# Expert weights of a mixture-of-experts stage: half of the raw pieces read into activation tiles, a strips read and a count sum moved to later places

## The chip, the cores and the metric

The kernel runs on one core of a Trainium2 chip. The metric is device time in microseconds for one launch, the median of several runs. The profile is of one execution on the same kind of chip; all positions in it are microseconds from the start of its span.

## The reference

Two transformer blocks run one after the other on 512 tokens of width 1024 (attention, recurrences and MLPs in the first; a delta-net layer and a sparse-attention layer in the second). Each of the two layers of the second block ends in a mixture of experts. This is the part that matters here:

```python
def hier_moe(x, w_grp, b_grp, w_rt, b_rt, w_gate, w_up, w_down):
    ...
    grp_prob, grp_idx = lax.top_k(grp_p, 1)
    ...
    top_p, top_i = lax.top_k(jax.nn.softmax(e_logits, axis=-1), MOE_TOP_K)
    ...
    def step(acc, e_in):
        wg, wu, wd, ge = e_in
        hdn = jax.nn.silu(xt @ wg) * (xt @ wu)
        return acc + ge[:, None] * (hdn @ wd).astype(jnp.float32), None

    y, _ = lax.scan(step, jnp.zeros((b * t, d), jnp.float32), (w_gate, w_up, w_down, gate.T))
```

There are 16 experts in 4 groups; each token goes to two experts of one group. The hidden width of an expert is 256.

## The kernel before, in words

**Numbers as pairs.** Matrix products are made from split numbers. `piece` (line 123) reads a raw piece of weights, 128 x 1024 f32 or 0.5 MB, into a raw tile (`ws`), ScalarE copies it to the rounded half `wh` (line 130), VectorE subtracts to get the rest `wl` (line 131), and `mm3` (line 148) makes three matmuls (lines 151 to 153) for each 128 x 128 block. A raw tile is free again when the subtraction is done. `wap` (line 135) yields the blocks of all pieces of a weight matrix in order.

**Tiles.** Tiles are taken by tag, each tag with a number of buffers (`BUFS`, line 17):

```python
BUFS = {"t": 6, "x": 16, "h": 4, "y": 10, "P": 3, "PT": 3, "bc": 2, "ws": 4, "wh": 3, "wl": 3}
```

So there are four raw tiles, three of each half, and ten activation tiles of tag `y`, of the same 4 KB per partition. In the mixture of layer 0 four `y` tiles hold the residual `z`, two hold the gain rows `G` and `Bv`, four are `ovx`, the space of the overflow path (`all_space`, line 1458), marked by small memsets and held until the branch; after the branch five are taken by the strips. In layer 1 `z` is in tag `h`, and the one-hot tiles are in `y`.

**Who orders the work.** The program is written straight down; a scheduler in the compiler orders the instructions of each engine and gives out the tiles, by the order of the program and by when it expects inputs and buffers to be ready. Nothing is ordered by hand. All loads and stores of these stages are issued by SP on one queue, in order, and a wait of one stops those behind it; the gathers of rows in `collect` are issued by GpSimd.

**The mixture** (`moe`, line 1305, called from `out_moe`). From the router's logits VectorE makes a 0/1 table `M` of tokens and experts. TensorE sums it in two ways: `pk` (lines 1339 to 1341), each token's position within its expert, and `pn` (line 1343), the number of tokens of each expert. The largest of these numbers (`mxf`, `mxi`, lines 1351 and 1352) is loaded by all engines (line 1377), and if it is above 128 the overflow path runs (lines 1378 and 1379). No instruction of that path stands in the trace. Experts run in pairs:

- `one_hot` (line 1519) makes a one-hot matrix of tokens and slots of two experts, and `gather` (line 1528) multiplies the split activations `Rs` with it, 16 matmuls of 256 columns for each of four parts; `dispatch` (line 1539) scales, shifts and splits the results. Of the first pair two parts are begun ahead of the branch (line 1375).
- `expert_up` (line 1556) multiplies by gate and up, eight blocks in four pieces, 24 matmuls of 512 columns, and makes the activation `eh`.
- `expert_down` (line 1567) transposes and splits it (`ehs`) and multiplies by down, two pieces and 12 matmuls of 512 columns; ScalarE copies the result to `ey` and SP stores it to a scratch `yd` in HBM (line 1588).

After seven pairs the rows are fetched back by token (`collect`, line 1450) and added to `z` with their weights (`add`, line 1418). The last pair stays on the chip and is added in `ln_out` (line 1218), which ends the layer with a norm whose gain row is `ln_ffn_g`.

**The strips** are tables of distance biases for the attention of layer 1. `strips_load` (line 1631) reads four strips and a companion `CB` from HBM into five `y` tiles; in the kernel before it is called right after the branch of layer 0 (line 1381).

Of the kernel before, what the change touches and what calls it, by code (L numbers as in the profile page):

```python
# [8 lines left out]
F32 = mybir.dt.float32  # L9
F32R = mybir.dt.float32r  # L10
I32 = mybir.dt.int32
AF = mybir.ActivationFunctionType
OP = mybir.AluOpType
AX = mybir.AxisListType
# [6 lines left out]
NT = 4  # L21
# [3 lines left out]
ORDER = (0, 1, 4, 5, 8, 9, 12, 13, 2, 6, 10, 14, 3, 7, 11, 15)  # L25
# [4 lines left out]
def rd(ap):  # L30
    return ap.bitcast(F32)


class Kern:
# [85 lines left out]
        self.nc.sync.dma_start(x, src)  # L120
        return x

    def piece(self, src, kp, cols, tag=None):
        nc = self.nc
        self.uid += 1
        new = lambda tag, dt: self.wp.tile([128, 1024], dt, tag=tag, name=f"{tag}_{self.uid}", bufs=BUFS[tag])[:, :kp * cols]
        ws = new("ws", F32)
        wh, wl = (self.T("w", tag, F32R)[:, :kp * cols] for _ in range(2)) if tag else (new("wh", F32R), new("wl", F32R))
        nc.sync.dma_start(ws, src)
        nc.scalar.activation(wh, ws, AF.Copy)  # L130
        nc.vector.tensor_tensor(wl, ws, rd(wh), op=OP.subtract)  # L131
        f = lambda x: x.rearrange("p (k c) -> p k c", k=kp)
        return f(wh), f(wl)

    def wap(self, name, kt, cols, off=0):

        a = self.A[name]
        kp = min(kt, 1024 // cols)

        def get(c, tag=None):  # L140
            for k in range(0, kt, kp):
                wh, wl = self.piece(a[off + c][:, k * cols:(k + kp) * cols], kp, cols, tag)
                for i in range(kp):
                    yield k + i, (wh[:, i], wl[:, i])

        return get
# [1158 lines left out]
    def moe(self, layer, lg, Rs, z, gain, parts):  # L1305
        nc = self.nc
# [26 lines left out]

        M = self.small((128, 64), "M", F32R, tag="m_M", bufs=1)
        M4 = M.rearrange("p (t g j) -> p t g j", t=NT, g=4)
        ALU(M4, A[0], A[1], OP.add)
        ALU(M4, rd(M4), og4, OP.mult)
        pk, pn = self.psum("pt"), self.psum("o")
        nc.tensor.matmul(pk[:, :64], self.mtri, M, start=True, stop=False)
        for t in range(1, NT):  # L1340
            nc.tensor.matmul(pk[:, 16 * t:64], self.onesr, M[:, :64 - 16 * t], start=False, stop=t == NT - 1)
        for t in range(NT):
            nc.tensor.matmul(pn[:, :16], self.onesr, M[:, 16 * t:16 * t + 16], start=t == 0, stop=t == NT - 1)
        M = rd(M)
        parts()

        pos = self.small((128, 64), "pos", tag="m_pos", bufs=1)
        nc.vector.scalar_tensor_tensor(pos, pk[:, :64], 1.0, M, op0=OP.add, op1=OP.mult)
        pos3 = pos.rearrange("p (t e) -> p t e", t=NT)
        mxf, mxi = self.small((128, 1), "mxf"), self.cp.tile([128, 1], I32, tag="mxi", name=f"mxi{layer}")  # L1350
        nc.vector.tensor_reduce(mxf, pn[:, :16], axis=AX.X, op=OP.max)
        nc.vector.tensor_copy(mxi, mxf)

        w1, wt = sm((), "w1"), sm((2,), "wt")
        for x in A:
# [16 lines left out]
        nc.vector.tensor_scalar(fits, pos3, float(CAP), None, op0=OP.is_le)  # L1372

        oh = self.one_hot(0, pos3, iota, "h" if layer == 0 else "y")
        begun = [self.gather(Rs, oh, r) for r in range(2)]
        space = self.all_space("h" if layer == 0 else "y")
        mx = nc.values_load(mxi[0:1, 0:1], min_val=0, max_val=S)
        with self.tc.If(mx > CAP):  # L1378
            self.overflow(layer, A, wt, fits, Rs, z, gain, space)
        if layer == 0:  # L1380
            self.strips_load()
        yd = self.yd[layer]
        xT = self.dispatch(layer, Rs, oh, begun)

# [19 lines left out]
        for c in range(2):  # L1404
# [7 lines left out]
            x, f = sm((16,), "ix"), sm((), "if")  # L1412
# [5 lines left out]
        def add(ys, w, t):  # L1418
            for c in (slice(0, S), slice(S, D)):
                nc.vector.scalar_tensor_tensor(z[t][:, c], ys[t][:, c], w[:, t:t + 1], z[t][:, c], op0=OP.mult, op1=OP.add)  # L1420

        for i in range(0, 16, 2):
# [4 lines left out]
            oh = self.one_hot(i + 2, pos3, iota, "h" if layer == 0 else "y")  # L1427
# [4 lines left out]
            if i == 12:  # L1432
# [10 lines left out]
                for t in range(NT):  # L1443
                    add(ys, wts[0], t)
        y = [self.expert_down(layer, 14 + e, h[e], None) for e in range(2)]
        for t in range(NT):
            add(yg, wts[1], t)
        return y, ohT, wlast
# [107 lines left out]
    def expert_up(self, layer, i, xT):  # L1556
        nc = self.nc
        pg = self.psum("s")
        for k, w in self.wap("moe_wgu", 8, 512)(layer * 16 + ORDER[i]):
            self.mm3(pg, tuple(a[:, i % 2] for a in xT[k]), w, k == 0, k == 7)  # L1560
        h = self.t("eh")
        nc.scalar.activation(h[:, :256], pg[:, :256], AF.Tanh, scale=0.5)
        nc.vector.scalar_tensor_tensor(h[:, :256], h[:, :256], 1.0, pg[:, :256], op0=OP.add, op1=OP.mult)
        nc.vector.scalar_tensor_tensor(h[:, 256:], h[:, :256], 0.5, pg[:, 256:], op0=OP.mult, op1=OP.mult)
        return h

    def expert_down(self, layer, i, h, yd):
        nc = self.nc
        pt = self.psum("pt")
        for j in range(2):  # L1570
            nc.tensor.transpose(pt[:, j * 128:(j + 1) * 128], h[:, 256 + j * 128:256 + (j + 1) * 128], self.ident)
        hs = self.t("ehs", F32R)
        self.split(pt[:, :256], hs[:, :256], hs[:, 256:])
        ps = [self.psum("lin") for _ in range(2)]
        for k, (wh, wl) in self.wap("moe_wd", 2, 1024)(layer * 16 + ORDER[i]):
            hk = hs[:, k * 128:(k + 1) * 128], hs[:, 256 + k * 128:256 + (k + 1) * 128]
            for hf in range(2):
                cs = slice(hf * S, (hf + 1) * S)
                self.mm3(ps[hf], hk, (wh[:, cs], wl[:, cs]), k == 0, k == 1)
        if yd is None:  # L1580
            y = [self.T("y", "x", F32R) for _ in range(2)]
            for hf in range(2):
                self.split(ps[hf], *(a[:, hf * S:(hf + 1) * S] for a in y))
            return y
        for hf, tag in enumerate(("P", "PT")):
            y = self.t("ey", tag=tag)
            nc.scalar.activation(y, ps[hf], AF.Copy)  # L1587
            nc.sync.dma_start(yd[1 + i * CAP:1 + (i + 1) * CAP, hf * S:(hf + 1) * S], y)
# [450 lines left out]
```

## Time and profile before

| | |
|---|---|
| median of 3 runs | 2843.3 us (2839.58 to 2848.86) |
| the profiled execution | 2845.23 us |
| its span | 2843.4 us, 40163 instructions |
| mean granted TensorE clock | 0.976 |
| PE busy | 2695.0 us (95%) |
| PE weight loads busy | 2302.5 us (81%) |
| VectorE busy | 1769.7 us (62%) |
| ScalarE busy | 1363.5 us (48%) |
| GpSimd busy | 182.0 us (6%) |
| DMA | 332.60 MB, mean 117 GB/s |
| gate-and-up pieces | 128 loads of 512 KB, median 4.9 us from issue to landing |
| down pieces | 64 loads of 512 KB, median 5.5 us |

How to read it: shares are of the whole span, in which the two expert stages are about a fifth. PE is TensorE, PEld its weight loads, ACT ScalarE, DVE VectorE, POOL GpSimd, SP the queue that issues the loads. A time in brackets is how long the engine stood idle just before an instruction, and behind the arrow is what released it. Matmuls are pipelined, so the recorded durations of neighbours overlap, and the distance of their starts is what one of them costs. An engine with a q (PEq, SPq) is its sequencer: it stands there for branches and for the issuing of transfers.

### The profile page before, as it was taken

To read this page: it belongs to the slowest core of one execution; us is meant where nothing else is said; L and a number is where in the kernel's file an instruction comes from. 1 tells how busy PE (TensorE), PEld (TensorE's weight loads), DVE (VectorE), ACT (ScalarE), POOL (GpSimd) and SP (SyncE) were. 2 spreads that over 40 slices of the span, in tenths; PEclk is the share of its full clock that TensorE was granted. 3 is DMA by queue.
4 is the path that set the end of the run, shared out by engine and by line. 5 is a ranking of instruction groups with operands and counts; after the bars stand their busy time and mean duration, and the time that the engine had idled before them with its cause. 6 is when DMAs were issued, how large, how long until landed. Compare 5 with 4: busy or idle time off the path is not lost. (4 is left out here: it accounts for less than half of the span.)

```text
span 2843.4 us, 40163 instructions
## 1 busy us (share of the span) xinstructions
PE 2695.0 (95%) x15128; PEld 2302.5 (81%) x15128; DVE 1769.7 (62%) x3583; ACT 1363.5 (48%) x2541; POOL 182.0 (6%) x185
## 2 busy tenths in 40 slices
PE   8999999999999999999999999979987999997995
PEld 6889888888888988888887888978776888896874
DVE  7675564444457655545446777668668377678767
ACT  5654442333356534422245444327774355535774
POOL 1101010000111010100001000000001011000001
PEclk9999999999999999999999999999998999998998
DMA  4314233333232421335333222327886211014885
GB/s 135 99 51 142 62 101 97 97 96 97 89 89 82 130 78 49 117 98 164 109 90 127 69 62 63 113 62 232 269 272 214 80 32 67 16 46 141 264 263 213
DMA packets 122535, 332.60 MB, mean 117 GB/s; under 512 B 21716, under 2 KB 37748, under 8 KB 122328
## 3 DMA queue, kind: packets, MB, share of 16 engines
q1 hardware_dynamic: 119896, 321.43, 36.1%
q0 software_dynamic: 2432, 8.46, 0.8%
q8 instruction: 124, 2.03, 0.3%
q14 instruction: 83, 0.68, 0.1%
HBM read 301.49 MB, written 28.02 MB: 116 GB/s over the span
## 5 line engine op out<-in xcount | busy, mean ns | idle before, releaser
L130 ACT ACTIVATE wh<-ws 128x1024 fp32r<-128x1024 f32 (+2 forms) x521 | 534.0, 1030 | 897.9 <-PE lin L152 599.5
L131 DVE TENSOR_TENSOR wl<-ws,wh 128x1024 fp32r<-128x1024 f32 (+2 forms) x521 | 617.0, 1191 | 221.6 <-ACT wh L130 220.6
L151 PE MATMUL lin<-xs,wh 128*128 128x512 f32 (+2 forms) x1080 | 429.0, 397 | 7.3 <-ACT xs L196 5.8
L152 PE MATMUL lin<-xs,wh 128*128 128x512 f32 (+2 forms) x1080 | 429.6, 398 | 2.5 <-DVE xs L197 2.5
L153 PE MATMUL lin<-xs,wl 128*128 128x512 f32 (+2 forms) x1080 | 428.6, 397 | 0.9 <-DVE wl L131 0.9
L151 PEld LDWEIGHTS lin<-xs,wh 128*128 128x128 f32 (+2 forms) x1080 | 203.3, 188 | 50.7 <-ACT xs L196 6.4
L152 PEld LDWEIGHTS lin<-xs,wh 128*128 128x128 f32 (+2 forms) x1080 | 203.2, 188 | 47.5 <-DVE xs L197 6.6
L153 PEld LDWEIGHTS lin<-xs,wl 128*128 128x128 f32 (+2 forms) x1080 | 203.3, 188 | 42.5 <-DVE wl L131 1.4
L346 DVE TENSOR_TENSOR h<-lin,h 128x512 f32<-128x512 f32 x112 | 77.4, 691 | 247.7 <-PE lin L153 247.5
L153 PE MATMUL lin<-sr,wl 128*128 128x512 f32 x512 | 199.3, 389 | 0.0
L152 PE MATMUL lin<-sr,wh 128*128 128x512 f32 x512 | 199.3, 389 | 0.0
L151 PE MATMUL lin<-sr,wh 128*128 128x512 f32 x512 | 199.2, 389 | 0.0
L733 DVE SCALAR_TENSOR_TENSOR ra<-lin,bc 128x512 f32<-128x512 f32 x64 | 44.2, 691 | 168.5 <-PE lin L153 165.9
L1535 PE MATMUL o<-oh,Rl 128*128 128x256 f32 x512 | 132.6, 290 | 7.2 <-PEq L1378 7.2
L304 ACT ACTIVATE P<-s,mn 128x256 f32<-128x256 f32 (+1 forms) x224 | 114.2, 514 | 52.7 <-DVE mn L302 50.0
L1535 PE MATMUL o<-oh,Rh 128*128 128x256 f32 x512 | 133.7, 293 | 4.9 <-issue 2.2
L152 PE MATMUL s<-wl,exh 128*128 128x512 f32 x256 | 107.4, 420 | 13.1 <-DVE wl L131 13.1
L151 PE MATMUL s<-wh,exh 128*128 128x512 f32 x256 | 103.0, 405 | 10.1 <-ACT wh L130 10.0
L152 PEld LDWEIGHTS lin<-sr,wh 128*128 128x128 f32 x512 | 96.1, 188 | 20.0
L151 PEld LDWEIGHTS lin<-sr,wh 128*128 128x128 f32 x512 | 96.1, 188 | 20.0
L153 PEld LDWEIGHTS lin<-sr,wl 128*128 128x128 f32 x512 | 96.1, 188 | 19.8
L1535 PEld LDWEIGHTS o<-oh,Rl 128*128 128x128 f32 x512 | 101.3, 198 | 13.3 <-issue 10.1
(605 smaller groups left out, 6178.4 us busy)
## 6 DMA issues: line engine op xcount, KB each, us to landing
ws<-in_moe_wgu SPq DMA_DIRECT2D x128, 512.0 KB, 4.9
ws<-in_mlp_wu SPq DMA_DIRECT2D x64, 512.0 KB, 3.6
ws<-in_mlp_wd SPq DMA_DIRECT2D x64, 512.0 KB, 3.6
ws<-in_moe_wd SPq DMA_DIRECT2D x64, 512.0 KB, 5.5
yd<-ey SPq DMA_DIRECT2D x56, 256.0 KB, 2.8
ws<-in_gdn_w SPq DMA_DIRECT2D x24, 512.0 KB, 3.6
ws<-in_ab_w SPq DMA_DIRECT2D x16, 512.0 KB, 4.3
ws<-in_xa_wk SPq DMA_DIRECT2D x16, 512.0 KB, 3.7
```

Source lines behind the costliest of these rows:

```text
L130: nc.scalar.activation(wh, ws, AF.Copy)
L131: nc.vector.tensor_tensor(wl, ws, rd(wh), op=OP.subtract)
L151: mm(out, a[0], b[0], start=start, stop=False)
L152: mm(out, a[0], b[1], start=False, stop=False)
L153: mm(out, a[1], b[0], start=False, stop=stop)
L304: nc.scalar.activation(P[:, :nk], p[:, :nk], AF.Exp, bias=mn, scale=-1.0, accum_out=den)
L346: self.nc.vector.tensor_tensor(self.hT[n], p, self.hT[n], op=OP.add)
L733: nc.vector.scalar_tensor_tensor(a, p, 0.0, rms()[1], op0=OP.max, op1=OP.mult)
L1535: self.nc.tensor.matmul(p[:, j * 256:(j + 1) * 256], Rs[t][i][:, fs], oh[:, t], start=t + i == 0, stop=t == NT - 1 and i == 1)
```

## The change

`piece` and `wap` get an argument for where a raw piece is read to. For the experts' weights, even pieces (0 and 2 of gate and up, 0 of down) are read to a tile of tag `y`, odd ones to a `ws` tile as before. `strips_load` is called after the down projection of the last pair of layer 0 and not after its branch. The sum `pn` and the two small instructions on it are moved from ahead of the one-hot to after it: the four matmuls stand between the first and the second begun gather, in a PSUM tile of tag `s` and not `o`, and the maximum after the second.

```diff
-    def piece(self, src, kp, cols, tag=None):
+    def piece(self, src, kp, cols, tag=None, raw="ws"):
...
-        ws = new("ws", F32)
+        ws = new("ws", F32) if raw == "ws" else self.T("ws", raw)[:, :kp * cols]
...
-    def wap(self, name, kt, cols, off=0):
+    def wap(self, name, kt, cols, off=0, raw=("ws",)):
...
-                wh, wl = self.piece(a[off + c][:, k * cols:(k + kp) * cols], kp, cols, tag)
+                wh, wl = self.piece(a[off + c][:, k * cols:(k + kp) * cols], kp, cols, tag, raw[k // kp % len(raw)])
...
-        pk, pn = self.psum("pt"), self.psum("o")
+        pk = self.psum("pt")
...
-        for t in range(NT):
-            nc.tensor.matmul(pn[:, :16], self.onesr, M[:, 16 * t:16 * t + 16], start=t == 0, stop=t == NT - 1)
-        M = rd(M)
+        Mr, M = M, rd(M)
...
-        mxf, mxi = self.small((128, 1), "mxf"), self.cp.tile([128, 1], I32, tag="mxi", name=f"mxi{layer}")
-        nc.vector.tensor_reduce(mxf, pn[:, :16], axis=AX.X, op=OP.max)
-        nc.vector.tensor_copy(mxi, mxf)
...
-        begun = [self.gather(Rs, oh, r) for r in range(2)]
+        begun = [self.gather(Rs, oh, 0)]
+
+        pn = self.psum("s")
+        for t in range(NT):
+            nc.tensor.matmul(pn[:, :16], self.onesr, Mr[:, 16 * t:16 * t + 16], start=t == 0, stop=t == NT - 1)
+        begun.append(self.gather(Rs, oh, 1))
+        mxf, mxi = self.small((128, 1), "mxf"), self.cp.tile([128, 1], I32, tag="mxi", name=f"mxi{layer}")
+        nc.vector.tensor_reduce(mxf, pn[:, :16], axis=AX.X, op=OP.max)
+        nc.vector.tensor_copy(mxi, mxf)
...
-        if layer == 0:
-            self.strips_load()
         yd = self.yd[layer]
...
         y = [self.expert_down(layer, 14 + e, h[e], None) for e in range(2)]
+        if layer == 0:
+            self.strips_load()
...
-        for k, w in self.wap("moe_wgu", 8, 512)(layer * 16 + ORDER[i]):
+        for k, w in self.wap("moe_wgu", 8, 512, raw=("y", "ws"))(layer * 16 + ORDER[i]):
...
-        for k, (wh, wl) in self.wap("moe_wd", 2, 1024)(layer * 16 + ORDER[i]):
+        for k, (wh, wl) in self.wap("moe_wd", 2, 1024, raw=("y", "ws"))(layer * 16 + ORDER[i]):
```

## Rows read from the trace of the kernel before

**Rows 1.** Windows: stretch, length; busy of PE, PEld, DVE, ACT, POOL; clock, DMA share, GB/s.

```profile
2676.00:2703.00 27.00, 25.36 (x140) 21.37 (x139) 18.70 (x22) 20.52 (x33) 0.00 (x0) 1.00 0.83 272
...
2758.00:2786.00 28.00, 24.50 (x128) 19.81 (x127) 18.85 (x23) 20.54 (x33) 5.47 (x4) 1.00 0.93 331
2786.00:2814.00 28.00, 18.53 (x66) 13.47 (x64) 22.01 (x28) 13.17 (x18) 7.54 (x4) 0.82 0.77 270
```

**Rows 2.** Timeline of PE in mid-stage: start, duration, engine, line, operation.

```profile
2677.19 0.39 PE L151 MATMUL s<-wh,exh 128*128 128x512 f32 x1
2677.42 0.28 PE L1535 MATMUL o<-oh,Rh 128*128 128x256 f32 x1
2677.54 0.28 PE L1535 MATMUL o<-oh,Rl 128*128 128x256 f32 x1
```

**Rows 3.** Timeline of SP: stores of a pair's second expert, six pairs apart, both layers.

```profile
1959.42 0.84 SPq L1588 DMA_DIRECT2D yd<-ey  x2
...
2130.87 1.16 SPq L1588 DMA_DIRECT2D yd<-ey  x2
...
2620.23 0.85 SPq L1588 DMA_DIRECT2D yd<-ey  x2
...
2785.85 0.81 SPq L1588 DMA_DIRECT2D yd<-ey  x2
```

**Rows 4.** Chain of waits within one pair of layer 1: start, duration, what.

```profile
2676.04 5.10 DMA ws<-in_moe_wgu
...
2683.59 4.41 DMA ws<-in_moe_wd
```

**Rows 5.** Waits of SP's queue, 2648 to 2758 (four pairs): us, times, longest.

```profile
SPq L129 <- DVE wl L131: 30.5, 28, 1.8
SPq L1588 <- ACT ey L1587: 25.4, 11, 3.5
```

**Rows 6.** Waits of ScalarE, the same stretch.

```profile
ACT wh L130 <- PE lin L153: 5.3, 4, 1.3
```

**Rows 7.** Last pair: chain of layer 1, and PE's timeline in both layers.

```profile
2797.97 9.17 DMA ws<-in_moe_wd
...
2152.74 0.80 PE L151 MATMUL lin<-wh,ehs 128*128 128x512 f32 x1 [4.23 <-ACT ehs L107]
...
2808.90 0.79 PE L151 MATMUL lin<-wh,ehs 128*128 128x512 f32 x1 [5.00 <-ACT ehs L107]
```

**Rows 8.** Timelines ahead of layer 0's first pair: SP, ACT, PE, POOL.

```profile
1856.04 44.44 SPq L129 DMA_DIRECT2D ws<-in_moe_wgu  x7
...
1896.44 1.06 ACT L130 ACTIVATE wh<-ws 128x1024 fp32r<-128x1024 f32 x1 [0.37 <-PE lin L153]
...
1930.70 0.40 PE L151 MATMUL s<-wh,exh 128*128 128x512 f32 x1
...
1830.60 0.10 POOL L1464 MEMSET ovx<- 128x2 f32 x1 [1.66 <-PE o L1098]
```

**Rows 9.** Timelines of PE and VectorE around the branch of layer 1.

```profile
2575.14 1.00 PE L1343 MATMUL o<-M,onesr 128*128 128x16 f32 x4
...
2576.18 0.17 DVE L1351 TENSOR_REDUCE mxf<-o 128x1 f32<-128x16 f32 x1 [0.63 <-PE o L1343]
...
2576.46 0.15 DVE L1352 CAST mxi<-mxf 128x1 int32<-128x1 f32 x1
...
2577.16 0.55 PE L1535 MATMUL o<-oh,Rh 128*128 128x256 f32 x1 [1.02 <-DVE oh L1524]
...
2582.15 0.55 PE L1535 MATMUL o<-oh,Rl 128*128 128x256 f32 x1 [3.58 <-PEq L1378]
```

**Rows 10.** Strips' reads, and the gain row's read and first use.

```profile
1919.61 3.39 SPq L1637 DMA_DIRECT2D strip<-skew  x4
...
2158.47 0.38 SPq L774 DMA_DIRECT2D ln_ffn_g<-in_ln_ffn_g  x1
...
L1241 DVE SCALAR_TENSOR_TENSOR R<-z,nm,ln_ffn_g x8: 1272/1277/1280, 2167.7 to 2832.9; 128x1024 f32<-128x1024 f32 x8
```

## The prediction, made before the changed kernel was run

> **What bounds the kernel now.** The edit touches only the two expert stages (layer 0 about 1900 to 2180 us, layer 1 about 2560 to 2843 us), so I read those, first by windows. In the middle of an expert stage TensorE is busy 25.4 us of 27 at the full clock and the DMA engines are busy for 0.83 of the time at 272 GB/s [rows 1]. Both look nearly full, so the next question is how much of that is real work. The PE timeline answers it: at the full clock one 512-column matmul follows another after 0.23 us and one 256-column gather after 0.12 us [rows 2], while the recorded durations (0.39 and 0.28) overlap. A pair of experts has 16 x 3 matmuls on the way up, 8 x 3 on the way down and 64 gathers: 72 x 0.23 + 64 x 0.12 = 24.2 us. The stores of the outputs mark the pairs in SP's queue: six pairs lie between the first two rows and six between the last two, so a pair takes 171.45 / 6 = 28.6 us in layer 0 and 165.62 / 6 = 27.6 us in layer 1 [rows 3]. So PE loses 4.4 and 3.4 us per pair.
>
> By the busy time of the first row PE is idle 1.6 us of the 27, and twelve pairs could win back 19 us at most. The Trainium skill (Perfetto Trace Analysis, Identifying the Most-Contended Engine) says that matmul occupancy is not a good measure of how near TensorE is to its limit and weight-load busy time is; that is 21.4 us in the same row, which would leave 5.6 us a pair. The count of matmuls lies between the two, and I go by the count.
>
> What ends last in a pair is read from the chain of waits: it passes twice through a load of raw weights, 5.10 us for a piece of gate-and-up and 4.41 us for a piece of down [rows 4]. These loads start late because SP waits: 30.5 us in four pairs until VectorE has split an old piece (the four raw tiles are all taken), and 25.4 us in front of stores whose ScalarE copy is not done [rows 5]. So the four raw tiles limit the read-ahead, and ScalarE, which works in order, stands still in front of a piece and delays the activations behind it.
>
> Is there bandwidth for more? A pair moves 12 x 0.524 MB of weights and 4 x 0.262 MB of outputs, 7.34 MB. The stretch with the row-gathers on a second queue shows 331 GB/s at a share of 0.93 [rows 1]: 7.34 MB would take 22.2 us, under the 24.2 of PE. DMA isn't the floor, though only 2 us below it.
>
> **The change, part by part.**
>
> Raw tiles. Pieces 0, 2 of gate-and-up and piece 0 of down go to the tag of ten activation tiles, the others to the four old ones. In layer 0 four of the ten are z, two the gain rows, and four the overflow space until the branch; after it those four are free because the strips no longer take them. So eight pieces can be under way instead of four; in layer 1, with two one-hots and the gain rows, up to ten. No instruction is added: the same loads, copies and subtractions. The gain is bounded by nothing and by the whole loss, 6 x 4.4 + 6 x 3.4 = 46.8 us. I take a pair of 26.2 us, leaving 2 us over the count, since not all stalls are of data: ScalarE also waits for a free split tile (5.3 us in four pairs [rows 6], three tiles per tag, unchanged), and the stores still stand in the loads' queue. That is (28.6 - 26.2) x 6 + (27.6 - 26.2) x 6 = 14.4 + 8.4 = 22.8 us.
>
> The last pair. Here the shortage is plainest: a down piece is on the chain for 9.17 us, and PE then waits 5.00 us for the activations (4.23 in layer 0) [rows 7]; the granted clock of that stretch is 0.82 [rows 1]. With eight or more tiles those pieces are asked for before the gathers of rows fill the DMA engines. VectorE is busy 22.0 of the stretch's 28 us, so it can shrink by 6 at most. Between 0 and 6 I take 5 per layer, being near to the wait that goes: 10 us.
>
> The first pair of layer 0. Now seven pieces are read ahead of the branch [rows 8], and some are split (the last copy at 1896.44), so the first matmul stands at 1930.70. Afterwards piece 0 wants an activation tile, and all ten are taken: the overflow tiles have been held since 1830.60 [rows 8]. It is issued only when SP has left the branch. If that comes late, at about 1924, then with 5.1 us of landing and a copy of 1.06 the first matmul stands at 1930.7 at best, and three copies that used to be done ahead (3.2 us) fall into this stretch. Ends: 0, and 8 if ScalarE has to do it all behind the gathers' outputs. I take 4, nearest to the three copies. In layer 1 the tiles of the branch outputs are free before the branch, and I count nothing.
>
> Counts summed late. VectorE's 0.63 us wait for the four count matmuls and its two small instructions (0.17 and 0.15) leave the path to the one-hot, so the first gather comes up to 0.9 us sooner; today it starts at 2577.16 [rows 9]. But the maximum now waits for sixteen gathers, estimated at half clock as 16 x 0.24 = 3.8 us, and the four count matmuls (1.00 us): 3.8 + 1.0 + 0.3 - 0.9 after today's first gather is 2581.4, 4.8 us later than now. PE today stands 3.58 us in the branch and resumes at 2582.15, 5.5 us after the maximum [rows 9]. Afterwards the wait falls behind one or two gathers instead of five matmuls, so the sum of PE's work and wait is nearly the same. Behind the wait on SP stand the weight loads, on ScalarE the gathers' outputs, on VectorE the slots. Ends: a gain of 2 and a loss of 4.8 per layer; I take a loss of 0.5, nearest to an even exchange: 1 us in all.
>
> Strips read later. The four reads took 3.39 us of SP at 1919.61 [rows 10], in a gap, so removing them is worth nothing there; the fifth held SP in mid-stage until the gain rows were used, which is inside the pairs' sum. All five issue now in the tail of layer 0, some 3.7 us of SP. Cover: the gain row of the last norm, issued at 2158.47, is first read at 2167.7 [rows 10], and the strips themselves only in the attention that follows. Nothing; 3.7 if they go ahead of that row.
>
> Sum: -22.8 - 10 + 4 + 1 = -27.8 us. Against the profiled execution, 2845.2 us (its span of 2843.4 and 1.8 around it), that is 2817.4. The median of the runs is 1.9 below the profiled one, so I give 2815.
>
> **The rivals.**
>
> The queue, not the tiles. The loads stay in one queue with the stores, and the 25.4 us in front of stores remain [rows 5], against 30.5 that go. If a load issued behind a blocked store is still the late one, a third of the pairs' gain is left (7.6) and half of the tail's (5): -12.6 + 5 = -8, 2835. For it: the store is on the chain right before the load [rows 4]. Against: with eight pieces ahead a stop of 3 us is no longer seen by ScalarE. The Trainium skill (Perfetto Trace Analysis, DMA Optimizations) advises one issuing engine for inputs and another for outputs, which this change doesn't do; that speaks for this rival, and no row of the old kernel shows the other arrangement. Chance 0.20.
>
> Slower: the late branch. All engines pass it, and no load into an activation tile of layer 0 can be issued before. If PE reaches it with nothing left to do, the whole 4.8 us are lost twice, the first pair costs its 8, and a read-ahead that starts empty regains only half of the queue rival's 12.6: 9.6 + 8 - 6.3 = +11, 2854. It decides when PE's first gather after the branch comes more than 4 us later than now counted from the position matmuls. Against it: today's wait of 3.58 us is already paid. Chance 0.11.
>
> All stalls go. Pairs at the matmul count plus 0.8, tails at 6: -(46.8 - 9.6) - 12 + 5 = -44, 2799. It needs every piece on time although ScalarE has only three split tiles. Chance 0.14. That the new tiles are not free at all, so nothing changes, would need the overflow tiles held past the branch; the code doesn't read them there. It goes into the queue rival.
>
> **How the numbers follow.** Forecast 0.55 (2806 to 2826), queue 0.20, all stalls 0.14, late branch 0.11. About 0.3% (8.5 us) is what a measurement of this kernel can tell from no change, that is 2835 and 2852. Faster: nearly all of the forecast, all of the third rival, half of the first: 0.78. Same: the other half of the first and a little of the branch: 0.12. Slower: 0.10. The outer ends of the bounds are 2780 (all pairs and tails at their best) and 2864; leaving out a tenth on each side gives 2788 to 2843.
>
> **What would show it.** Right: SP's waits for the splits of old pieces shrink from 30 us in four pairs to a few; pairs between stores fall to near 26 us in both layers; the copies no longer wait for the loads; the DMA rate in mid-stage rises to about 280 GB/s; PE's wait before the last pairs' down matmuls falls from 4 to 5 us to under 2. Wrong: pairs still at 27 us or more, with the copies waiting for split tiles or loads behind stores; or a first matmul of layer 0's experts more than 8 us later after the position matmuls.

## The result, and the profile after

The changed kernel takes 2800.63 us in the median of 6 runs (2793.84 to 2802.98). The kernel before, run beside it on the same chips, takes 2846.08 us (6 runs, 2839.58 to 2854.26). The ratio is 0.9826 with a 95% interval of 0.981 to 0.9842, so by the ratio the change saves 45 to 54 us; the two medians lie 45.5 us apart. The profiled execution took 2798.65 us, its span is 2796.9 us. The forecast was 2815, and the range 2788 to 2843.

**Where the time went** is read first by dividing the span at marks that both kernels have: the position matmul ahead of each branch, the second store of the first and of the seventh pair, and the first store of the layer's norm (in layer 1 the end of the span).

| us | before | after | difference |
|---|---|---|---|
| layer 0: position matmul to second store of pair 1 | 47.8 | 49.4 | +1.6 |
| layer 0: six pairs | 171.5 | 150.6 | -20.9 |
| layer 0: last pair to first store of the norm | 47.4 | 41.8 | -5.6 |
| between the two expert stages (not edited) | 396.0 | 395.6 | -0.4 |
| layer 1: position matmul to second store of pair 1 | 46.0 | 47.8 | +1.8 |
| layer 1: six pairs | 165.6 | 151.0 | -14.6 |
| layer 1: last pair to the end | 57.5 | 49.1 | -8.4 |

The sum is -46.5 us, and the spans differ by 2843.4 - 2796.9 = 46.5. Nearly all of the gain lies in the pairs and the last pairs, and the starts of both layers have become a little longer. Here are the stores that bound the six pairs, in SP's timeline; they answer to [rows 3].

```profile
1961.03 0.81 SPq L1592 DMA_DIRECT2D yd<-ey  x2
...
2111.60 0.92 SPq L1592 DMA_DIRECT2D yd<-ey  x2
...
2596.79 0.81 SPq L1592 DMA_DIRECT2D yd<-ey  x2
...
2747.78 0.82 SPq L1592 DMA_DIRECT2D yd<-ey  x2
```

That is 150.57 / 6 = 25.1 us per pair in layer 0 and 150.99 / 6 = 25.2 in layer 1, where it was 28.6 and 27.6. The two layers are now alike. The time of a pair before is less certain than that of a pair now: in the profile of e3 below, which does not touch layer 1, layer 1's pairs take 28.8 us and not 27.6.

**What bounds a pair now.** The windows of the mid-stage (stretch, length; busy of PE, PEld, DVE, ACT, POOL; clock, DMA share, GB/s) answer to [rows 1]:

```profile
2050.00:2075.00 25.00, 25.00 (x142) 21.39 (x141) 19.10 (x22) 21.49 (x34) 0.00 (x0) 1.00 0.87 296
2648.00:2673.00 25.00, 25.00 (x141) 21.30 (x140) 20.25 (x27) 21.31 (x33) 0.00 (x0) 1.00 0.90 315
2698.00:2723.00 25.00, 25.00 (x142) 21.43 (x141) 20.30 (x27) 21.29 (x33) 0.00 (x0) 1.00 0.88 295
2748.00:2776.00 28.00, 23.94 (x99) 16.93 (x99) 27.69 (x40) 13.68 (x20) 7.80 (x4) 1.00 0.51 169
```

TensorE is busy in every microsecond of the first three, at the full clock; the DMA rate rose from 272 to about 300 GB/s. The fourth is the last pair of layer 1: VectorE is busy 27.7 of 28 us there, where before the DMA engines stood at a share of 0.93 and 0.77 [rows 1].

**The waits** of four pairs of layer 1 (us in total, times, longest). First what ScalarE's copies waited for in the kernel before, in the stretch of [rows 5] and [rows 6]:

```profile
ACT wh L130 <- DMA ws<-in_moe_wgu: 13.2, 10, 2.9
...
ACT wh L130 <- DMA ws<-in_moe_wd: 2.4, 3, 1.9
```

Then the changed kernel, 2622 to 2723, the computing engines and SP's queue, the latter against [rows 5]:

```profile
DVE wl L131 <- ACT wh L130: 8.5, 16, 1.3
...
ACT wh L130 <- PE lin L154: 5.8, 9, 1.2
ACT wh L130 <- PE s L154: 4.5, 12, 0.9
```

```profile
SPq L129 <- DVE wl L131: 36.0, 16, 5.4
SPq L129 <- DVE eh L1567: 14.9, 8, 2.6
SPq L1592 <- ACT ey L1591: 11.6, 8, 4.2
```

Two things are to be seen. In this stretch no line has a copy (`wh`) waiting for a load any more, where it was 15.6 us; ScalarE waits for TensorE to give split tiles back, which is what an engine ahead of the slowest one does. And SP still waits as long for old pieces to be split as before, 36.0 us against 30.5, but in 16 waits and not 28. A wait of the loads' queue tells nothing by itself: before, a load was late when it came, and now it waits for a tile that will be needed some pieces later. That the loads are under way longer (page part 6: gate-and-up pieces 5.9 us from issue to landing, 4.9 before; stores 4.7, 2.8 before) costs nothing in this stretch either, since no engine waits for them.

**The start of a layer.** Three rows of SP's and PE's timelines of layer 0, against [rows 8]; the brackets hold the idle time ahead and what ended it:

```profile
1857.01 12.79 SPq L129 DMA_DIRECT2D ws<-in_moe_wgu  x4
...
1923.53 1.92 SPq L129 DMA_DIRECT2D ws<-in_moe_wgu  x4
```

```profile
1921.99 0.36 PE L1539 MATMUL o<-oh,Rh 128*128 128x256 f32 x1 [1.53 <-PEq L1382]
...
1929.37 0.79 PE L152 MATMUL s<-wh,exh 128*128 128x512 f32 x1 [3.07 <-ACT wh L130]
```

Ahead of the branch SP now issues four pieces and not seven. The next ones, piece 0 among them, come at 1923.53, 1.5 us after the branch, and the first matmul of the experts waits 3.07 us for the copy of such a piece. It stands 17.8 us after the position matmul (1911.61), where it stood at 19.05: the branch itself costs PE 1.53 us of idle time where it cost 3.66, and part of the late load is paid by that. The second store comes 1.6 us later all the same, so the rest of the first pair loses 2.9 us more. In layer 1 the first matmul comes early (13.8 us after the position matmul, 17.5 before), but then PE stands five times before the second store, 5.0 us in all; its waits in 2562 to 2598, and what ScalarE waits for there:

```profile
PE s L153 <- DVE wl L131: 1.7, 2, 1.0
PE o L1539 <- ACT ex L1555: 1.7, 1, 1.7
PE s L152 <- ACT wh L130: 0.9, 1, 0.9
PE lin L152 <- ACT ehs L107: 0.7, 1, 0.7
```

```profile
ACT wh L130 <- DMA ws<-in_moe_wd: 1.9, 1, 1.9
...
ACT wh L130 <- DMA ws<-in_moe_wgu: 1.0, 1, 1.0
```

Here copies still wait for loads: the read-ahead is not yet built up. In layer 1, too, SP stands in front of the branch. The program takes the overflow space there as well, six `y` tiles (GpSimd marks them from 2521.68), SP has issued five pieces by 2513.1, and the next come behind the branch, 9.9 us after the position matmul (2549.02):

```profile
2558.96 1.72 SPq L129 DMA_DIRECT2D ws<-in_moe_wgu  x3
```

Behind the last three of PE's waits the granted clock is 0.50 from 2592 to 2594, and the long matmuls there stand 0.43 us apart and not 0.23, so the waits cost more than their 5.0 us.

**The counts.** VectorE's timeline of layer 0, against [rows 9] (layer 1):

```profile
1913.52 0.17 DVE L1378 TENSOR_REDUCE mxf<-s 128x1 f32<-128x16 f32 x1 [0.54 <-PE s L1375]
...
1913.78 1.42 DVE L1528 TENSOR_TENSOR oh<-c_moe,pos 128x256 fp32r<-128x256 f32 x4
1915.12 0.15 DVE L1379 CAST mxi<-mxf 128x1 int32<-128x1 f32 x1
```

The scheduler did not follow the order of the text. The four count matmuls stand at 1912.48, the same place as before, and the maximum still stands ahead of the one-hot; only the cast went behind it. It comes 3.5 us after the position matmul, where it came 2.2 after it. And 32 gathers now stand ahead of the branch and not 5, so PE has work while the count is being loaded. The branch itself is left later. VectorE's first instruction behind it, before and after:

```profile
1917.76 0.23 DVE L1307 TENSOR_TENSOR row<-pos,c_moe 128x64 f32<-128x64 f32 x1 [2.31 <-DVEq L1378]
...
1923.45 0.22 DVE L1308 TENSOR_TENSOR ix<-first,e2e 128x64 f32<-128x64 f32 x1 [2.91 <-DVEq L1382]
```

That is 6.1 us after the position matmul before and 11.8 after; SP's first issue behind the branch comes 8.0 and 11.9 us after it. The loads that had to wait for the branch thus start 4 us later.

### The profile page after: what moved, and what is told of

Read it like the earlier page. It is cut to its first block, busy times and chain, and to the rows that moved or that the text cites. A ratio compares the mean times of both kernels' runs of the same rounds, so it can differ in the third digit from the quotient of the medians.

```text
span 2796.9 us, 40163 instructions
## 1 busy us (share of the span) xinstructions
PE 2682.8 (96%) x15128; PEld 2294.2 (82%) x15128; DVE 1770.3 (63%) x3583; ACT 1367.6 (49%) x2541; POOL 181.9 (7%) x185
## 5 line engine op out<-in xcount | busy, mean ns | idle before, releaser
L153 PEld LDWEIGHTS lin<-xs,wh 128*128 128x128 f32 (+2 forms) x1080 | 203.0, 188 | 47.6 <-DVE xs L198 7.1
L313 PE MATMUL o<-c_ident,P 128*128 128x128 f32 x536 | 97.0, 282 | 12.2 <-ACT P L305 11.4
L1539 PEld LDWEIGHTS o<-oh,Rh 128*128 128x128 f32 x512 | 101.7, 199 | 8.6 <-ACT ex L1555 4.1
```

What stands on the lines that cost most here:

```text
L153: mm(out, a[0], b[1], start=False, stop=False)
L313: nc.tensor.transpose(pt[:, b * 128:(b + 1) * 128], P[:, b * 128:(b + 1) * 128], self.ident)
L1539: self.nc.tensor.matmul(p[:, j * 256:(j + 1) * 256], Rs[t][i][:, fs], oh[:, t], start=t + i == 0, stop=t == NT - 1 and i == 1)
```

## The experiments

Ratios are to the kernel before, run beside each, with 95% intervals. "Start" is position matmul to second store of the first pair, "pair" is the mean of six between stores, for layer 0 and layer 1.

| | median us | ratio | start | pair |
|---|---|---|---|---|
| kernel before | 2846.1 | | 47.8, 46.0 | 28.6, 27.6 |
| changed kernel | 2800.6 | 0.9826 [0.9810, 0.9842] | 49.4, 47.8 | 25.1, 25.2 |
| e1_counts_early | 2797.5 | 0.9826 [0.9796, 0.9855] | 47.8, 43.8 | 25.1, 25.1 |
| e2_counts_late_only | 2845.9 | 0.9982 [0.9961, 1.0003] | 44.4, 43.7 | 28.3, 28.7 |
| e3_strips_late_only | 2850.2 | 0.9998 [0.9978, 1.0018] | 48.2, 45.7 | 28.4, 28.8 |
| e4_stores_act | 2885.3 | 1.0141 [1.0116, 1.0166] | 48.1, 47.7 | 30.3, 30.7 |
| e5_first_ws | 2792.5 | 0.9785 [0.9771, 0.9798] | 42.9, 43.2 | 25.1, 24.9 |
| e6_two_mm_before | 2853.4 | 1.0014 [0.9998, 1.0030] | 47.6, 44.1 | 27.5, 29.7 |
| e7_two_mm_after | 2764.6 | 0.9694 [0.9677, 0.9712] | 45.4, 46.6 | 22.6, 23.0 |
| e8_all_y | 2799.6 | 0.9817 [0.9798, 0.9836] | 49.3, 46.3 | 25.7, 25.2 |
| e9_first_ws_counts_early | 2792.4 | 0.9807 [0.9787, 0.9828] | 45.3, 43.8 | 25.0, 25.0 |
| e10_no_adds | 2786.1 | 0.9790 [0.9770, 0.9810] | 42.6, 43.3 | 25.1, 24.9 |

Starts and pairs are of one profile each. Where two kernels have the same code they repeat like this: starts within 0.4 us (layer 1 of the kernel before and of e3, both layers of e5 and e10), pairs within 0.1 us in e5 and e10, but 1.2 us apart in layer 1 of the kernel before and of e3.

**The three parts, one at a time.** e1 takes the late counts back out of the changed kernel, e2 and e3 put one part alone into the kernel before.

```diff
# e1: in the changed kernel (e2: the reverse, in the kernel before)
-        pk = self.psum("pt")
+        pk, pn = self.psum("pt"), self.psum("o")
...
-        begun = [self.gather(Rs, oh, 0)]
...
+        begun = [self.gather(Rs, oh, r) for r in range(2)]
# e3: in the kernel before
-        if layer == 0:
-            self.strips_load()
         yd = self.yd[layer]
...
         y = [self.expert_down(layer, 14 + e, h[e], None) for e in range(2)]
+        if layer == 0:
+            self.strips_load()
```

> The changed kernel with the count sum put back ahead of the one-hot; raw tiles and strips stay changed. Theory A (read-ahead of raw pieces carries the gain): pairs stay at 25.1 us in both layers and the time stays within 5 us of the changed kernel's 2800.6, a ratio to the kernel before of 0.982 to 0.986; PE stands about 3.6 us in the branch again after five gathers, and in exchange the loads behind the branch start about 4 us sooner, so the first pair ends at nearly the same time. Theory B (the late count carries a good part): over 10 us slower than the changed kernel, ratio above 0.986.

> The kernel before with only the count sum moved. Theory A: pairs unchanged at 27.6 to 28.6 us; only the start of a layer moves, the block of 64 gathers ending up to 4 us sooner per layer: ratio 0.997 to 1.000. Theory B: a ratio under 0.995.

> The kernel before with only the strips read later. Theory A: the raw tiles are four as before, so layer 1 is unchanged and layer 0's pairs stay over 27.4 us; ratio 0.998 to 1.002. Rival C (the fifth strip read, which holds SP in the third pair, and the 2 MB of strips cost layer 0 its longer pairs): layer 0's pairs fall by 1 us or more and the ratio is under 0.998.

Late strips alone are worth nothing (0.9998), and late counts alone 0.2%, with an interval from 0.4% to no change. Taking the late counts out of the changed kernel leaves the same ratio, 0.9826, and the same pairs. So it is the tiles that carry the gain; in layer 1, which reads no strips, they do it alone (27.6 to 25.1 us in e1). The starts move all the same: e2's are 3.3 and 2.3 us shorter than those of the kernel before, and e1's are 1.6 and 4.0 us shorter than those of the changed kernel. What that means is taken up below, with e9. e3 also shows that freeing four `y` tiles does nothing as long as no raw piece is read to them. That the late strips give the read-ahead its room in layer 0 once the pieces go there is argued from the tiles and was not tried.

**The queue or the tiles.** In the kernel before, the stores of the experts' outputs go to another engine's queue, so that no load stands behind a store that waits.

```diff
-            nc.sync.dma_start(yd[1 + i * CAP:1 + (i + 1) * CAP, hf * S:(hf + 1) * S], y)
+            nc.scalar.dma_start(yd[1 + i * CAP:1 + (i + 1) * CAP, hf * S:(hf + 1) * S], y)
```

> The kernel before with the stores of the experts' outputs issued from ScalarE's queue, so that no load stands behind a store that waits. Theory A (four raw tiles are the limit): a load still waits for the split of the piece four back, pairs stay above 27 us, ratio 0.996 to 1.004. Rival D (the queue is the limit): pairs fall to 25 to 26 us and most of the 45 us are found here too, ratio 0.983 to 0.990.

It got slower by 1.4%, with pairs of 30.3 and 30.7 us. SP's waits and ScalarE's, 2660 to 2770, and one window:

```profile
SPq L129 <- DVE wl L131: 83.2, 37, 9.3
SPq L129 <- DVE eh L1563: 12.8, 7, 2.1
```

```profile
ACT wh L130 <- DMA ws<-in_moe_wgu: 17.6, 15, 2.7
ACT wh L130 <- DMA ws<-in_moe_wd: 7.5, 7, 1.6
```

```profile
2685.00:2710.00 25.00, 22.80 (x124) 18.50 (x123) 15.71 (x17) 16.69 (x25) 0.00 (x0) 1.00 0.71 235
```

With the stores gone from its queue SP stands all that time in front of the four raw tiles, and the copies wait for loads as before. So taking away the stop in front of stores did not help as long as there were four raw tiles. By itself this run doesn't clear the queue, for the edit also gives ScalarE more to do; the changed kernel does, in which the stores stand in SP's queue as before and the pairs fall to 25.1 us. Why e4 is slower and not the same isn't settled: the stores land 6.8 us after issue (2.8 before, page part 6), and ScalarE, which every piece passes, now issues them too, at 0.83 us for two.

**What sets a pair, before and after.** Both kernels leave out the product of the rounded weights with the rest of the activations on the way up, 16 of a pair's 72 long matmuls; at 0.23 us each [rows 2] that is 3.7 us of PE.

```diff
-            self.mm3(pg, tuple(a[:, i % 2] for a in xT[k]), w, k == 0, k == 7)
+            x = tuple(a[:, i % 2] for a in xT[k])
+            nc.tensor.matmul(pg, x[0], w[0], start=k == 0, stop=False)
+            nc.tensor.matmul(pg, x[0], w[1], start=False, stop=k == 7)
```

> The kernel before with one of the three matmuls of each block left out on the way up (the product with the activations' rest): TensorE has 16 x 0.23 = 3.7 us less in a pair. Theory A (the four raw tiles set the pair): pairs shrink by less than 1.2 us, to 26.5 us or more. Rival (TensorE sets it already): pairs shrink by over 3 us.

> The changed kernel with the same product left out. Theory A (TensorE sets the pair now, 25.1 us): pairs shrink to 22.3 to 23.5 us, where the DMA engines' 22.2 us come next. Rival (loads or ScalarE set it still): less than 1 us.

Taken from the kernel before, 3.7 of a pair's 24.2 us of matmuls are worth nothing (1.0014); its pairs went 1.1 us down in layer 0 and 2.1 us up in layer 1, and why up is open. Taken from the changed kernel they are worth 36 us (2800.6 - 2764.6): pairs of 22.6 and 23.0, 2.5 and 2.2 us less. The second stores of e7, SP's timeline:

```profile
1952.53 0.81 SPq L1594 DMA_DIRECT2D yd<-ey  x2
...
2088.05 0.81 SPq L1594 DMA_DIRECT2D yd<-ey  x2
```

This is the plainest evidence in the study: the bound moved from the read-ahead to TensorE. It also tells that the next one is near. Of the 3.7 us only 2.2 to 2.5 come out. Which it is stays open: the 22.2 us of transfers that the prediction worked out from the highest DMA rate are just below, but in e7's mid-stage (2000 to 2045) ScalarE is busy 41.9 of 45 us too, with the DMA engines at a share of 0.92, and in its layer 0 pairs PE waits 7.1 us for ScalarE's `ehs` while copies wait only 2.1 us for loads.

**How much read-ahead, and in which tiles.** All experts' pieces go to `y` tiles and none to the four old ones, or (e5) those of a layer's first expert only to the old ones.

```diff
# e8, both calls
-raw=("y", "ws")
+raw=("y",)
# e5, gate and up only
-        for k, w in self.wap("moe_wgu", 8, 512, raw=("y", "ws"))(layer * 16 + ORDER[i]):
+        for k, w in self.wap("moe_wgu", 8, 512, raw=("y", "ws") if i else ("ws",))(layer * 16 + ORDER[i]):
```

> The changed kernel with every expert piece in an activation tile and none in the four old raw tiles: in layer 0 four tiles again until the gain rows are free, six in layer 1. Theory A (the number of tiles counts, not which they are): layer 0's pairs go back above 27 us in its first half, layer 1's lie between 25.1 and 27; time between 2812 and 2840. Rival (the place or the order of the loads counts): pairs stay at 25.1 in both.

The time is that of the changed kernel, so which tags the tiles come from is of little account. Layer 0 shows the number that it takes. While `z` and the gain rows still hold six of the ten tiles, four are left, and the first of the six pairs takes 27.5 us; `rescale` is run early in the stage, six and more are free from about 1970, and the next pair takes 24.6. Second stores of e8, layer 0:

```profile
1954.13 0.81 SPq L1592 DMA_DIRECT2D yd<-ey  x2
...
1981.66 0.82 SPq L1592 DMA_DIRECT2D yd<-ey  x2
...
2006.24 0.81 SPq L1592 DMA_DIRECT2D yd<-ey  x2
```

So four tiles leave a pair near where it was; this rests on one pair, the same that takes 26.1 us in the changed kernel. Six seem enough: layer 1, which by the program has six, has the changed kernel's pairs (25.2). Neither theory came whole: Theory A's long pairs came once and its time did not come, and the rival's 25.1 us came in layer 1 only.

> The changed kernel, but the four gate-and-up pieces of the first expert of each layer go to the four old raw tiles, which are free ahead of the branch. Theory E (the start of a layer lost 1.6 to 1.8 us because piece 0 waits for an activation tile that is held until the branch, and its load then shows as 3.1 us of idle TensorE in layer 0): the first matmul on weights follows the last gather without a gap, the second store of the first pair comes 3 to 5 us sooner after the position sum in each layer, pairs stay 25.1, time 2791 to 2796, ratio 0.979 to 0.981. Rival (the start is bound by the branch and by ScalarE's order, not by the load): unchanged, ratio 0.982 to 0.984.

This is the best version, faster than both kernels. SP's timeline ahead of layer 0's experts, and PE's first matmul:

```profile
1854.30 42.87 SPq L129 DMA_DIRECT2D ws<-in_moe_wgu  x6
1898.43 0.33 SPq L129 DMA_DIRECT2D ws<-in_moe_wd  x1
...
1922.13 1.03 SPq L129 DMA_DIRECT2D ws<-in_moe_wgu  x2
```

```profile
1924.38 0.40 PE L152 MATMUL s<-wh,exh 128*128 128x512 f32 x1
```

Six pieces and one of down are issued ahead of the branch, the first matmul waits for none and stands 14.5 us after the position matmul (1909.93), against 17.8 in the changed kernel. In layer 1 it stands where it did (13.7 us), but a down piece is read ahead of the branch there too, and PE's waits up to the second store are 1.2 us and not 5.0. The starts shrink to 42.9 and 43.2 us, by 6.5 and 4.6, while the pairs stay. The loss at the start of both layers was thus late pieces of the first pair, and it is not a price that the change has to pay: it is gone when the first expert keeps to tiles that are free ahead of the branch.

**The counts once more.** In e1 the late first piece could hide what the counts are worth, so they were tried on e5, where it is gone (the edit is that of e1).

> The changed kernel with two edits: the first expert of a layer reads all its up-projection pieces into the split tiles, as in e5_first_ws, and the sum of the counts stands ahead of the one-hot again, as in e1_counts_early. Theory A: the late counts were worth nothing in e1 only because the first matmul of a layer waited for piece 0; with piece 0 read ahead of the branch that cover is gone, and the shorter idle time at the branch (1.5 and 0.7 us against 3.6 and 3.7 us) should count: 2 to 3 us per layer slower than e5 (2792.5), so 2797 to 2799 us. Theory B: the branch's idle time is taken from the gathers that follow anyway, so the counts are worth nothing here either: 2791 to 2794 us, with first stages (count matmul to second store) of 43 us in both layers, as in e5.

The stages show what the time can't: starts of 45.3 and 43.8 us against 42.9 and 43.2, first matmuls 18.5 and 17.0 us after the position matmul against 14.5 and 13.7. PE's wait in the branch is back, layer 0 in e9:

```profile
1916.42 0.55 PE L1536 MATMUL o<-oh,Rl 128*128 128x256 f32 x1 [3.37 <-PEq L1379]
```

By the starts the late counts are worth 2.4 and 0.6 us here. The first matmul gains more (4.0 and 3.3), and part of it is given back before the second store. Theory B has the time and Theory A the starts, in size for layer 0 only. The medians are equal (2792.4 and 2792.5), and the ratios' intervals overlap: 3 us are less than half the width of either (about 8 and 12 us).

With e1 and e2 the starts make a table, and it shows that what the late counts are worth hangs on where the first pieces are read:

| start in us, layer 0 and layer 1 | counts early | counts late | late counts |
|---|---|---|---|
| four raw tiles (kernel before, e2) | 47.8, 46.0 | 44.4, 43.7 | -3.3, -2.3 |
| even pieces in `y` tiles (e1, changed kernel) | 47.8, 43.8 | 49.4, 47.8 | +1.6, +4.0 |
| the same, a layer's first expert in the old tiles (e9, e5) | 45.3, 43.8 | 42.9, 43.2 | -2.4, -0.6 |

Late counts let the gathers run ahead of the branch, and the branch is left later. Where the first pieces are read ahead of it, that is a gain. In the changed kernel pieces of the first expert stand behind it: SP's first issue after the branch comes 11.9 us after the position matmul in layer 0 and 9.9 in layer 1, in e1 8.1 and 7.7, and PE has no wait for data between the branch and layer 1's second store in e1, where it has 5.0 us of them in the changed kernel. So in the changed kernel itself the late counts are a loss at the start, and e5 turns them into a gain.

**The last pair.** On top of e5, the additions of the collected rows cover 16 columns and not twice 512, which leaves out nearly all of the sum over the first fourteen experts.

```diff
-            for c in (slice(0, S), slice(S, D)):
-                nc.vector.scalar_tensor_tensor(z[t][:, c], ys[t][:, c], w[:, t:t + 1], z[t][:, c], op0=OP.mult, op1=OP.add)
+            c = slice(0, 16)
+            nc.vector.scalar_tensor_tensor(z[t][:, c], ys[t][:, c], w[:, t:t + 1], z[t][:, c], op0=OP.mult, op1=OP.add)
```

> The kernel of e5_first_ws with the weighted additions of the collected rows of the first fourteen experts cut from 2 x 512 columns to 16 columns: the sixteen instructions of 0.74 us per layer become sixteen short... eight of about 0.2 us, so VectorE loses some 10 us of work per layer. It leaves out nearly all of the sum over those experts. Theory A: the tail of a layer is bound by VectorE since the loads no longer bound it (in the last 28 us of experts VectorE was busy 27.7 us, TensorE 23.9): the tail shortens by 5 us or more per layer, 2775 to 2783 us. Theory B: the tail is bound by the collecting of rows by GpSimd or by the loads: the additions only fill time, under 1 us per layer, 2790 to 2793 us.

Neither theory holds for both layers. The tail (seventh second store to the norm's first store, or the end) goes from 42.2 to 41.3 us in layer 0 and from 49.1 to 47.0 in layer 1: 3 us for 16 us of VectorE's work (1768.1 us busy in e5, 1751.8 in e10, page part 1). Layer 0's 0.9 us lies within Theory B, layer 1's 2.0 in neither. The rest of the difference is not in these stages: in the profiles 4.7 us of it lie ahead of layer 0's position matmul, which no edit touches. The chain of e5 in its last stretch holds additions, that of e10 doesn't, and it tells why so little comes out (e5's line first):

```profile
2741.71 1.97 DVE z L1422 x3
...
2736.14 4.69 DMA yd<-ey
...
2741.61 6.40 DMA yg<-yd,ii
2748.18 1.22 DVE wl L131
```

In e10 the chain goes through the store of the last outputs, their collection by row, and the splits of the last pieces, work that the additions had run beside. A VectorE that is busy 27.7 of 28 us looks like the bound of the tail; what it holds up is worth 1 to 2 us, since store, collection and TensorE end almost as late.

## Why the prediction was right, and where it was off

**Raw tiles: right in the mechanism, too small in size.** Four raw tiles limited the read-ahead, and that was the bound of the pair: e6 shows that TensorE was not, the waits of the copies (15.6 us in four pairs, none after) that late loads were, and the changed kernel, with its stores still in the loads' queue, that the queue was not. The term was -22.8 us, and -35.5 was measured (20.9 + 14.6), with the uncertainty that layer 1's pairs before have. The step that failed is "I take a pair of 26.2 us, leaving 2 us over the count, since not all stalls are of data: ScalarE also waits for a free split tile ..., and the stores still stand in the loads' queue". Both waits are still there after (5.8 us for split tiles in four pairs, 11.6 in front of stores), and they cost TensorE nothing: with six or more pieces ahead each is over before the piece is needed. The pair came to 25.1 and 25.2, the matmul count plus 1 us. That was the price of the rival "all stalls go" (2799 us), which is what happened. What would have told it: a wait of ScalarE for PE to return a split tile is no loss of PE.

**How full TensorE was.** The busy time of PE [rows 1] left 1.6 us of 27 to gain, and the count left 3 and more; the time between the stores fell by 3.5 and 2.4 us per pair, so the busy time understated it, as the prediction took it. The Trainium skill (Perfetto Trace Analysis, Identifying the Most-Contended Engine) says that matmul occupancy is not a good measure of how close TensorE is to its roofline, and names two others in its place, the share of peak FLOPs that the matmuls reach and weight-load busy time. The trace agrees with the first half: TensorE was busy 25.4 of 27 us [rows 1], and 2.4 to 3.5 us of a pair came out all the same. Of the two others the prediction quoted only weight-load busy time, and that alone would say that 3.6 us in 25 are still free, for it is 21.4 now. The runs don't bear that out: PE has no wait for data in the four pairs, and the pair follows TensorE's work (e7). The count of matmuls by their spacing was the measure that held.

**The last pair: right.** -10 was given and -14.0 measured (5.6 and 8.4). The down pieces are issued before the last rows are collected, all but one in layer 1 (2754.79, the collecting begins at 2753.80): PE's wait before the last pair's down matmuls is 0.64 us in both layers where it was 4.23 and 5.00 [rows 7]. The bound that "it can shrink by 6 at most" was too low for layer 1: it was taken from VectorE's work in one window of 28 us, and the last pair of that layer lasts 57.5. VectorE is busy 25.3 of the 29 us behind that window, so it stood idle 9.7 us in the whole.

**The first pair: nearly right in sum, by luck.** +4 was given for layer 0 alone, "I count nothing" for layer 1, and +1 for the counts in both, +5 in all. Measured were +1.6 and +1.8, counts included. The parts were off and offset each other. The raw tiles, set against e2, which has the late counts too, cost 5.0 us in layer 0 (44.4 to 49.4) and 4.1 in layer 1 (43.7 to 47.8). In layer 0 the cause is the one named, a first piece late behind the branch, sized about right at 4, and e5 takes it away. In layer 1 the step that failed is the nothing that was counted because "the tiles of the branch outputs are free before the branch": the overflow space takes six of the ten `y` tiles in that layer too, SP issues five pieces and then stands until 2558.96, and PE waits 5.0 us for what comes behind. With early counts (e1) the same five pieces are enough, and layer 1's start is 43.8 us.

**Counts summed late: the branch left later as forecast, by another way, and the price mis-sized.** The maximum was to be there "4.8 us later than now", since it was to wait for sixteen gathers. It did not wait: the scheduler left it ahead of the one-hot, and only the cast moved, by 1.3 us. Yet VectorE left the branch 5.7 us and SP 4.0 us later against the position matmul. Which of the moved instructions does that was not tried apart. PE's own wait shrank, with 32 gathers ahead of the branch (1.53 and 0.66 us, from 3.66 and 3.58). A loss of 0.5 us per layer was taken, as an even exchange. It is none: with four raw tiles the late counts gain 3.3 and 2.3 us (e2), and in the changed kernel they lose 1.6 and 4.0 (e1), because the weight loads stand behind the branch there, which the prediction named ("Behind the wait on SP stand the weight loads") and gave no price.

**Strips: right.** They are issued one by one between 2103.16 and 2126.14, the gain row follows at 2131.72, and nobody waits for either.

**The rivals.** "The queue, not the tiles" fell with the pairs of 25.1 us, which came with the stores still in the loads' queue. The Trainium skill (Perfetto Trace Analysis, DMA Optimizations) says that it may make sense, especially with loops or control flow, to give inputs to one issuing engine and outputs to another. In e4 that brought no gain: with the stores on ScalarE's queue the kernel before was 1.4% slower. "The late branch" was to decide when PE's first gather behind the branch comes more than 4 us later; it comes 10.4 us after the position matmul and came 7.9 after it, 2.5 later. Its mechanism, loads that cannot be issued before the branch, was there, at the 1.6 and 4.0 us of e1. One sign given for a right forecast was wrong though the forecast was not: SP's waits for old pieces did not shrink (36.0 us). The other signs came: pairs near 25, no copy waiting for a load in mid-stage, about 300 GB/s, 0.64 us in the last pair.

## What to carry to other kernels

When TensorE, DMA and the queue all look nearly full, leave out a part of TensorE's work once: if the time stays, something else sets the pace. If copies then wait for loads and the loads' queue for tiles, as here, more tiles to read ahead are the first thing to try. Tiles of another tag that are idle in a stage served as well as the old ones here, but look at what holds them at the stage's start: the first pieces do best in tiles that are free before the branch. And try each part of a change with and without the others: the late counts gained with one arrangement of tiles and lost with another. Size the gain by the next engine's own count of work, and count a wait only if the bounding engine, not the queue, is the one that waits.

## What the hardware showed beside this

- **The clock around the branch.** In the changed kernel TensorE's granted clock was 0.50 while the first gathers ran and 1.00 right behind them, still ahead of the branch, after it had stood 7.97 us in front of the position matmul and then worked for some 7 us. Windows of layer 0, columns as above:

```profile
1914.30:1918.70 4.40, 4.35 (x20) 4.38 (x21) 2.97 (x15) 0.57 (x2) 0.00 (x0) 0.50 0.00 2
1919.10:1921.00 1.90, 1.36 (x12) 1.16 (x10) 0.69 (x1) 1.19 (x4) 0.00 (x0) 1.00 0.05 13
```

  That is 1.2 and then 2.4 GHz. In the kernel before, with five gathers and then the wait of 3.66 us ahead of the branch, the granted clock is still 0.50 from 1919.50 to 1925.50 and 1.00 from 1925.70, while the last gathers run. So the low clock meets 20 gathers in the changed kernel and 22 in the kernel before, and in both the experts begin at full clock: running gathers ahead of the branch fills the wait, but saves hardly any of them from the low clock.
- **Loads under way at once.** With six or more half-megabyte pieces ahead, the same queue and engines carried 295 to 315 GB/s in mid-stage where four gave 272. That is what the shorter pair moves: 7.34 MB in 25.1 us are 292 GB/s. A gate-and-up piece took 1 us longer to land (median 4.9 to 5.9), a down piece hardly (5.5 to 5.6).
- **The parts that no edit touched.** The sparse attention between the two expert stages took from 394 to 404 us in the profiles of these kernels, and layer 0's position matmul stood between 1904.8 and 1911.7. Nothing in the study explains it, and differences of a few microseconds between medians stay open for that reason.
